# A decoder layer on one core: shorter ways at five places, and the merge's gates loaded ahead

## The chip, the core and the metric

The kernel runs on one core of one Trainium2 chip. A core has five engines, each with its own list of instructions that it takes in order: TensorE (PE, matmuls into the PSUM banks), VectorE (DVE), ScalarE (ACT), GpSimd (POOL, which here works on SBUF only) and SyncE (SP, which here issues most of the transfers). Engines wait for one another by semaphores. The metric is the device time of one execution in microseconds (us).

## The reference

One decoder layer over 1,024 tokens of width 1,024, in float32. Two mixers read the same normalised input: sparse attention over 8 heads (a compressed, a selected and a sliding-window branch) and gated linear attention (GLA) over 4 heads. Their outputs are projected, gated and summed, and a gated channel mixer follows. Cut to what matters here:

```python
h = rmsnorm(x, norm_mix[layer])
proj = h @ w_in[layer]
q_nsa, kv_nsa, g_nsa, q_gla, k_gla, v_gla, lr_gla, r_gla, g_merge = split_in_proj(proj)
k_cmp = compress_blocks(kv[0], ...)          # and v_cmp
o_a = nsa_attention(q_a, k_cmp, v_cmp, kv[2], kv[3], kv[4], kv[5], gates_a)
o_b = gla_chunked(q, k, v, log_a)            # then rmsnorm, times silu(r_gla)
gate_a, gate_b = jnp.split(jax.nn.sigmoid(g_merge), 2, axis=-1)
merged = gate_a * (o_a @ w_up_nsa[layer]) + gate_b * (o_b @ w_up_gla[layer])
x = x + merged @ w_out[layer]
h = rmsnorm(x, norm_ffn[layer])
x = x + (jax.nn.silu(h @ w_ffn_gate[layer]) * (h @ w_ffn_up[layer])) @ w_ffn_down[layer]
return rmsnorm(x, norm_final)
```

## The kernel before

Everything is held transposed: channels on the 128 partitions, tokens along the free dimension, in two halves of 512 tokens (`hf`). Each float32 product of the projections is three matmuls over a high and a low part of each operand (`wh`, `wl`, `hh`, `hl`): high by high, high by low, low by high. A weight tile `wf` is loaded by SP, ACT copies its high part to `wh`, and POOL subtracts to get `wl` (`part` and `half_weights`, L351 to L364); three such tiles are held at a time. `products` (L401) is one such product over the eight or four blocks of 128 channels, and L410 its matmul.

**Order.** PE's list is written by hand, in program order. The lists of the other engines are set at build time by a scheduler, from estimated times; instructions inside `keep_in_program_order` keep their place. A `Fill` is a queue of small items (a product of three matmuls, cost 648 for eight-channel blocks, or a load with cost 0), which the stages take from in between their own work.

**Stages, in order of time.**

1. *Head, to about 173 us.* The input comes in and is split; PE begins with the first columns of queries and keys of GLA. The sum of squares of every token is formed by matmuls with a matrix of ones, and its inverse root `rbc` has one token per column, the same on all partitions (`first_roots`, L571, with `rms_root`). `root_turned` (L579) makes `rtok`, with tokens on the partitions, by eight products of one row by a single one. `rtok` scales the values and the GLA inputs that have tokens on partitions, from about 112 us on. Behind the first projections come the compression jobs: DVE sums a bias `pb` over sixteen blocks of the weights `w1` (L627, L629), and `hidden` multiplies (L638).
2. *GLA, to about 300.* Eight chunks of 128 tokens. For each, `gla_prep` makes decayed copies for seven levels (POOL subtracts, ACT exponentiates, DVE multiplies into `xq`, L828), `gla_diag` the diagonal, `gla_level` a level (PE L859, into one of three banks; DVE copies from it under a mask, L861). `gla_stream` yields a cost after each, and the loop at the end takes fill items for that cost times `ratio`, which spreads the whole fill over the stream.
3. *Sparse attention, 366 to about 777.* 16 units of two groups by eight query blocks, group 0 from the last block down, group 1 upwards. `Plan` writes PE's order by hand from estimated ready times: scores, turns of the weights, value products, with fill in the gaps. All of a unit's value products collect in the one bank `o` (L1165, L1182). `finish` (L1188) copies its upper half to SBUF on ACT (`fo`, L1195), and DVE adds lower half and copy into `oa` (L1197). In `Plan`, `self.o` is when the bank is expected to be free. The fill here is 14 merge-gate projections (stored to `zd`) and five of the eight projections of GLA's output (`UP`, stored to `ud`).
4. *Merge, 783 to about 848.* For eight blocks `m` and two halves: 12 matmuls where `m` is in `UP`, else 24. The evacuation (L1269) loads the two gate halves `za` and `zb`, and `u` where `m` is in `UP`, takes the sigmoid (L1276, L1277), multiplies and adds (L1279 to L1283), and splits the sum into high and low part (`mg`, L1285 and L1286). Then the output projection and the channel mixer follow.
5. *Channel mixer, to the end.* At the end, the last half of the tokens comes in two parts of 320 and 192 columns: `plus` adds the products to the residual (L1588), `square` and `roots` make the last inverse root, and `store` scales (L1602) and stores.

Buffers are rings by tag. `big` has 18 buffers of 4 KB a partition, `prob` 4 of 4 KB, and `mid` 10 of 2 KB.

## Time and profile before

| | us |
|---|---|
| median of three timed runs | 1596.46 |
| the three runs | 1596.6, 1596.46, 1591.89 |
| the profiled execution | 1600.53 |
| its span, first to last instruction | 1598.7 |
| PE busy in the span | 1567.5 (98%) |
| DVE, ACT, POOL busy | 1010.4, 814.4, 678.3 |
| granted clock of PE, mean | 0.998 of full speed |

The profile is of one execution, which took 4.1 us more than the median of the timed runs. A busy PE is one with a matmul under way; what it waits for is found from the semaphores. Times in rows are microseconds from the span's start, unless a column says ns.

### The profile page before, as it was taken

What the parts mean: (1) busy time and instruction counts of PE and PEld (TensorE: products, weight loads), DVE (VectorE), ACT (ScalarE), POOL (GpSimd) and SP (SyncE); (2) the same over time, 40 slices, a digit from 0 to 9 for tenths busy, and PEclk for the clock granted to TensorE, in tenths of its full rate; (3) what the DMA queues carried; (4) which work ended last, traced back from release to release, by engine and by line L of the source; (5) the groups of instructions that cost most, each with busy time, mean ns of one, the idle gap of its engine ahead of it and who ended that gap; (6) DMA issues with size and microseconds to landing.
All of it is one profiled execution on the core that took longest, in us unless ns stands there. A gap on an engine that the chain in (4) does not pass through costs nothing.

```text
span 1598.7 us, 23059 instructions
## 1 busy us (share of the span) xinstructions
PE 1567.5 (98%) x8047; PEld 1311.5 (82%) x8047; DVE 1010.4 (63%) x1653; ACT 814.4 (51%) x1632; POOL 678.3 (42%) x590
## 2 busy tenths in 40 slices
PE   9999999999999999999999999999999999999998
PEld 7888988888888888888877878888888888888887
DVE  7681487586777677677564477744444444499785
ACT  6241555575676676677653344433433444454542
POOL 6110366562212233130144440466666666556570
PEclk9999999999999999999999999999999999999999
DMA  5431112232112122131466532323323323695423
GB/s 182 132 102 61 60 53 68 96 106 83 46 52 65 62 77 65 45 109 60 138 210 206 192 116 73 119 99 106 104 101 105 105 99 99 240 362 162 140 72 125
DMA packets 109590, 179.85 MB, mean 112 GB/s; under 512 B 12689, under 2 KB 29730, under 8 KB 109474
## 3 DMA queue, kind: packets, MB, share of 16 engines
q1 hardware_dynamic: 105442, 171.95, 32.8%
q10 hardware_dynamic: 4032, 6.44, 1.1%
q8 instruction: 63, 1.03, 0.3%
q14 instruction: 53, 0.43, 0.1%
HBM read 128.27 MB, written 45.88 MB: 109 GB/s over the span
## 4 chain that ended last, share of the span: by engine, by line
PE 82%; DVE 6%; DMA 4%; ACT 3%; issue 3%; POOL 2%; SPq 0%; DVEq 0%; POOLq 0%; ACTq 0%
PE m L410 12%; PE d L410 10%; PE m L1397 9%; PE m L1398 9%; PE m L1396 9%; PE m L1759 4%; PE m L1760 4%; PE m L1758 4%; PE o L1182 3%; PE t L1173 3%; PE s L1094 2%; PE s L1095 2%; PE t L725 1%; PE t L726 1%; PE t L727 1%
## 5 line engine op out<-in xcount | busy, mean ns | idle before, releaser
L357 POOL TENSOR_TENSOR wl<-wf,wh 128x512 fp32r<-128x512 f32 x106 | 145.1, 1371 | 323.7 <-ACT wh L356 312.5
L1396 PE MATMUL m<-xt,wh 128*128 128x512 f32 x412 | 160.3, 389 | 0.0
L1397 PE MATMUL m<-xt,wh 128*128 128x512 f32 x412 | 160.3, 389 | 0.0
L1398 PE MATMUL m<-xt,wl 128*128 128x512 f32 x412 | 160.3, 389 | 0.0
L1326 POOL TENSOR_TENSOR wl<-ws,wh 128x512 fp32r<-128x512 f32 x76 | 107.5, 1419 | 73.4 <-ACT wh L1325 73.4
L1151 DVE TENSOR_TENSOR ptl<-t,pth 128x512 fp32r<-128x512 f32 (+1 forms) x168 | 99.4, 596 | 35.5 <-ACT pth L1150 32.5
L1326 POOL TENSOR_TENSOR wl<-wr,wh 128x512 fp32r<-128x512 f32 x69 | 92.2, 1337 | 69.6 <-ACT wh L1325 69.6
L1325 ACT ACTIVATE wh<-ws 128x512 fp32r<-128x512 f32 x76 | 48.0, 632 | 131.4 <-PE m L1397 114.7
L1150 ACT ACTIVATE pth<-t 128x512 fp32r<-128x512 f32 (+1 forms) x168 | 88.0, 525 | 52.8 <-PE t L1173 46.9
L1325 ACT ACTIVATE wh<-wr 128x512 fp32r<-128x512 f32 x87 | 55.0, 632 | 116.9 <-POOL wl L1326 76.4
L1758 PE MATMUL m<-xb,wh 128*128 128x512 f32 x280 | 109.5, 391 | 0.3 <-DVE g L1458 0.3
L1759 PE MATMUL m<-xb,wh 128*128 128x512 f32 x280 | 109.0, 389 | 0.0
L1760 PE MATMUL m<-xb,wl 128*128 128x512 f32 x280 | 108.9, 389 | 0.0
L1326 POOL TENSOR_TENSOR wl<-wd,wh 128x512 fp32r<-128x512 f32 x56 | 82.8, 1482 | 58.3 <-ACT wh L1325 54.7
L410 PE MATMUL m<-hh,wh 128*128 128x512 f32 x240 | 100.4, 419 | 0.0
L1326 DVE TENSOR_TENSOR xb<-ar,xb 128x512 fp32r<-128x512 f32 x73 | 80.3, 1117 | 31.8 <-ACT xb L1325 31.8
L410 PE MATMUL m<-hh,wl 128*128 128x512 f32 x240 | 93.8, 391 | 0.0
L410 PE MATMUL m<-hl,wh 128*128 128x512 f32 x240 | 93.7, 390 | 0.0
L356 ACT ACTIVATE wh<-wf 128x512 fp32r<-128x512 f32 x106 | 65.9, 625 | 53.6 <-PE m L410 25.1
L1396 PEld LDWEIGHTS m<-xt,wh 128*128 128x128 f32 x412 | 77.3, 188 | 16.2
L1398 PEld LDWEIGHTS m<-xt,wl 128*128 128x128 f32 x412 | 77.3, 188 | 16.0
L1397 PEld LDWEIGHTS m<-xt,wh 128*128 128x128 f32 x412 | 77.3, 188 | 16.0
(414 smaller groups left out, 4545.5 us busy)
## 6 DMA issues: line engine op xcount, KB each, us to landing
ar<-actd SPq DMA_DIRECT2D x77, 256.0 KB, 2.8
wf<-in_w_t SPq DMA_DIRECT2D x58, 256.0 KB, 2.9
wr<-in_w_gate SPq DMA_DIRECT2D x44, 256.0 KB, 2.7
wr<-in_w_upf SPq DMA_DIRECT2D x44, 256.0 KB, 2.7
wd<-in_w_down SPq DMA_DIRECT2D x33, 256.0 KB, 5.2
zd<-zt SPq DMA_DIRECT2D x32, 256.0 KB, 2.0
wf<-in_w_out SPq DMA_DIRECT2D x32, 256.0 KB, 3.2
actd<-t SPq DMA_DIRECT2D x30, 256.0 KB, 2.0
```

Source lines behind the costliest of these rows:

```text
L357: (eng or V).tensor_tensor(wl, wf, f(wh), OP.subtract)
L410: PE.matmul(st["p"], w, x, start=k + i == 0, stop=k == n - 1 and i == 2)
L1150: S.activation(th[:, :c], pt[:, :c], AF.Copy)
L1151: V.tensor_tensor(tl[:, :c], pt[:, :c], f(th[:, :c]), OP.subtract)
L1325: S.activation(th, src, AF.Copy)
L1326: eng.tensor_tensor(tl, src, f(th), OP.subtract)
L1396: PE.matmul(ps, wh[:, c], xh, start=first and k == 0, stop=False, skip_group_check=not first)
L1397: PE.matmul(ps, wh[:, c], xl, start=False, stop=False, skip_group_check=not first)
L1398: PE.matmul(ps, wl[:, c], xh, start=False, stop=k == MH - 1, skip_group_check=not first)
L1758: PE.matmul(dst, wh[:, c], xh, start=first and p == 0, stop=False, skip_group_check=not first)
L1759: PE.matmul(dst, wh[:, c], xl, start=False, stop=False, skip_group_check=not first)
L1760: PE.matmul(dst, wl[:, c], xh, start=False, stop=p == NP - 1, skip_group_check=not first)
```

## The change

Six edits. (1) The first roots come behind seven items of the first work list instead of five; three of these items are loads, so four products stand before them instead of two. (2) `root_turned` stores one partition of `rbc` to memory and loads it back with tokens on the partitions; PE and a PSUM bank have no part in it. (3) In GLA 1,200 is added to the cost behind each diagonal, and to the whole by which `ratio` divides. (4) In `finish`, but for the last unit, DVE copies the lower half of the bank to SBUF beside ACT's copy, and POOL adds the two copies; the planner expects the bank back when the later of the two copies is done. For group 0, POOL also makes the high and low parts of `oa`, before the work of ACT and DVE. (5) In the merge, the gate halves of one block and half come as one load into a tile of the ring `big`, three halves ahead, `u` for both halves of a block as one load into the ring `prob`, and one sigmoid covers both gates, in program order. (6) Three of the eight stores of the second to last part are put behind the last additions.

```diff
@@ -101,7 +101,7 @@
 LAT, WAIT, LOADED, COPIED = 155.0, 300.0, 1500.0, 3000.0
 NBIG, NMID, NSMALL = 18, 10, 8
 SCRATCH = 2048
-FINE, NGATE = 3, 2
+FINE, NGATE, AHEAD = 3, 2, 1200
 
 UP = (1, 2, 4, 5, 7)
 
@@ -212,9 +212,7 @@
         later()
         self.t += 218.0 * n if b.br else 436.0
         if last and b.br == 2 and b.j == 1:
-            t = self.on("A", self.t, 478.0)
-            t = self.on("D", t, 670.0)
-            self.o = t + LAT
+            self.o = max(self.on("A", self.t, 478.0), self.on("D", self.t, 550.0)) + LAT
 
     def run(self):
         ops = dict(T=(self.turn_at, self.turn), S=(self.score_at, self.score), P=(self.value_at, self.value))
@@ -576,11 +574,11 @@
         for n in (2, 3, 4, 5, 0, 1):
             scaled(dst[n], acc[n] if n > 1 else dst[n], n % 2, 0.125 if n < 4 else None)
 
+    rtd = dr.tile([1, T], F32, name="rtd")
+
     def root_turned():
-        ps = ps_o()
-        for b in range(NB):
-            PE.matmul(ps[:, b:b + 1], rbc[0:1, bs(b)], ones[0:1, 0:1], start=True, stop=True)
-        V.tensor_copy(rtok, ps[:, :NB])
+        load(rtd, rbc[0:1, :])
+        load(rtok, rtd.rearrange("o (b p) -> p (o b)", p=128))
 
     def proj(evac, bank=ps_m, fine=False):
 
@@ -733,7 +731,7 @@
     j1, h1, t1, s1 = compress_job(1)
     lb, wb = token_weights(a["w_b"], 512, 2)
     work = dense([(a["w_t"][3], proj(lambda p, hf: scaled(kg[hf][:, 1, :], p, hf))), j0, key_job(0), j1, key_job(1)], ready=first)
-    fill.add(work[:5] + [(900.0, first_roots), (0.0, load_consts)] + work[5:20] + [(400.0, root_turned)] + work[20:48] + h0 + work[48:59] + t0
+    fill.add(work[:7] + [(900.0, first_roots), (0.0, load_consts)] + work[7:20] + [(0.0, root_turned)] + work[20:48] + h0 + work[48:59] + t0
              + work[59:63] + s0 + work[63:69] + lb[:1] + work[69:74] + lb[1:2] + work[74:84] + h1 + lb[2:] + work[84:])
     fill.flush()
 
@@ -909,7 +907,7 @@
     def gla_stream():
         for c in range(NB):
             gla_diag(c)
-            yield 860
+            yield 860 + AHEAD
             for i in range(NLV):
                 gla_level(c, i)
                 yield 430
@@ -952,7 +950,7 @@
         return a["w_t"][8 + 2 * g + j], proj(lambda p, hf: scaled(qr[g][hf][:, j, :], p, hf, 0.125))
 
     fill.add(dense([query_job(0, 0), query_job(0, 1)] + [gate_job(j) for j in range(NGATE)]))
-    ratio = fill.cost() / (8 * (860 + 7 * 430 + 3220) + 1500)
+    ratio = fill.cost() / (8 * (860 + AHEAD + 7 * 430 + 3220) + 1500)
     for cost in gla_stream():
         fill.run(cost * ratio)
     fill.flush()
@@ -1191,12 +1189,18 @@
             hf = i // 4
             if oa[g][hf] is None:
                 oa[g][hf] = big("oa", shape=(2, 512))
-            fo = mid("fo")
+            fo, end = mid("fo"), (g, i) == units[-1]
             S.activation(fo[0:64, :], po[64:128, :], AF.Copy)
+            if not end:
+
+                t = mid("fp")
+                tc.keep_in_program_order(V.tensor_copy(t[0:64, :], po[0:64, :]))
+                po = t
             for par in range(2):
-                V.tensor_add(oa[g][hf][64 * par:64 * par + 64, :, bs(i % 4)],
-                             po[0:64, :].rearrange("p (j r q) -> p j r q", j=2, r=2)[:, :, par, :],
-                             fo[0:64, :].rearrange("p (j r q) -> p j r q", j=2, r=2)[:, :, par, :])
+                (V if end else P).tensor_tensor(
+                    oa[g][hf][64 * par:64 * par + 64, :, bs(i % 4)],
+                    po[0:64, :].rearrange("p (j r q) -> p j r q", j=2, r=2)[:, :, par, :],
+                    fo[0:64, :].rearrange("p (j r q) -> p j r q", j=2, r=2)[:, :, par, :], OP.add)
             del UN[g, i]
 
 
@@ -1249,11 +1253,32 @@
         for j in range(2):
             th, tl = big("oah", F32R), big("oal", F32R)
             for hf in range(2):
-                S.activation(th[:, hs(hf)], oa[g][hf][:, j, :], AF.Copy)
-                V.tensor_tensor(tl[:, hs(hf)], oa[g][hf][:, j, :], f(th[:, hs(hf)]), OP.subtract)
+                if g:
+                    S.activation(th[:, hs(hf)], oa[g][hf][:, j, :], AF.Copy)
+                else:
+                    P.tensor_copy(th[:, hs(hf)], oa[g][hf][:, j, :])
+                (V if g else P).tensor_tensor(tl[:, hs(hf)], oa[g][hf][:, j, :], f(th[:, hs(hf)]), OP.subtract)
             oah.append(th)
             oal.append(tl)
+
+
+    fetched, US = {}, {}
+    halves = deque((m, hf) for m in range(NM) for hf in range(2))
+
+    def fetch():
+        if halves:
+            m, hf = halves.popleft()
+            t = big("zz", shape=(2, 512))
+            SP.dma_start(t, zd.rearrange("(a m) p t -> m p a t", a=2)[m][:, :, hs(hf)])
+            if m in UP and hf == 0:
+                US[m] = prob("u")
+                SP.dma_start(US[m], ud[m])
+            fetched[m, hf] = t, US.get(m)
+
+    for _ in range(2):
+        fetch()
     fill.flush()
+    fetch()
 
 
     psum("pp3", m=7, o=1)
@@ -1267,16 +1292,12 @@
                     ps[hf] = p
 
                 def evac(p, hf=hf):
-                    za, zb = mid("za"), mid("zb")
-                    SP.dma_start(za, zd[m, :, hs(hf)])
-                    SP.dma_start(zb, zd[8 + m, :, hs(hf)])
+                    zz, u = fetched.pop((m, hf))
+                    za, zb = zz[:, 0, :], zz[:, 1, :]
+                    fetch()
+                    tc.keep_in_program_order(S.activation(zz, zz, AF.Sigmoid))
                     if m in UP:
-                        u = mid("u")
-                        SP.dma_start(u, ud[m, :, hs(hf)])
-                    S.activation(za, za, AF.Sigmoid)
-                    S.activation(zb, zb, AF.Sigmoid)
-                    if m in UP:
-                        P.tensor_tensor(zb, u, zb, OP.mult)
+                        P.tensor_tensor(zb, u[:, hs(hf)], zb, OP.mult)
                     else:
                         V.tensor_mul(zb, ps[hf], zb)
                     V.tensor_mul(za, za, p)
@@ -1596,10 +1617,12 @@
         else:
             sums[n].append(sq)
 
-    def store(blk, mp, hf, c=slice(0, 512)):
+    def store(blk, mp, hf, c=slice(0, 512), late=False):
         m = mp + (MH if blk[0] == "2" else 0)
         xv, at = x1[blk, mp][:, c], slice(512 * hf + c.start, 512 * hf + c.stop)
-        V.scalar_tensor_tensor(xv, xv, gains[:, 2, m:m + 1], rbc[:, at], op0=OP.mult, op1=OP.mult)
+        ins = V.scalar_tensor_tensor(xv, xv, gains[:, 2, m:m + 1], rbc[:, at], op0=OP.mult, op1=OP.mult)
+        if late:
+            tc.keep_in_program_order(ins)
         (S if c.start and mp % 2 else SP).dma_start(outT[:, m, at], xv)
 
 
@@ -1717,7 +1740,9 @@
         when(i + 2, roots, 0, H[h])
         when(i + 2, sums[0].__delitem__, slice(1, None))
         for k in range(2 * MH):
-            when(i + 5 + k // 2, store, "12"[k // MH] + "1", k % MH, 0, H[h])
+
+            late = h == 0 and k > MH
+            when(i + (NP - ALL + 2 if late else 5 + k // 2), store, "12"[k // MH] + "1", k % MH, 0, H[h], late)
 
     with tc.manual_schedule(engines={mybir.EngineType.SP}):
         for i in range(3):
```

SP's list at the head, behind the input's loads. `wf` are weight tiles, `cst` the constants, `w` and `pe` the compression weights. Before:

```order
L355 DMA wf<-in_w_t 128x512 x3
L497 DMA cst_471<-in_consts 128x768
L497 DMA cst_476<-in_consts 128x448
L610 DMA w_573<-in_cmp_w 128x1024
L610 DMA w_574<-in_cmp_w 128x1024
L497 DMA w_577<-in_cmp_w 128x128
L497 DMA pe<-in_cmp_pe 128x16
L355 DMA wf<-in_w_t 128x512 x2
```

With the change:

```order
L353 DMA wf<-in_w_t 128x512 x4
L495 DMA rtd<-rbc 1x1024
L495 DMA cst_478<-in_consts 128x768
L495 DMA cst_483<-in_consts 128x448
L495 DMA rtok<-rtd 128x8x1
L608 DMA w_566<-in_cmp_w 128x1024
L608 DMA w_567<-in_cmp_w 128x1024
L495 DMA w_570<-in_cmp_w 128x128
L495 DMA pe<-in_cmp_pe 128x16
L353 DMA wf<-in_w_t 128x512
```

One weight load has moved ahead of the constants, and the store and the load of the root stand before and behind them; the compression weights come after both.

SP's list where the attention ends and the merge begins. `zd` and `ud` are the stored gates and projections, `za`, `zb`, `zz` and `u` their tiles. Before:

```order
L355 DMA wf<-in_w_up 128x512
L1215 DMA ud<-zt 128x512
L1271 DMA za<-zd 128x512
L1272 DMA zb<-zd 128x512
L1271 DMA za<-zd 128x512
L1215 DMA ud<-zt 128x512
L1272 DMA zb<-zd 128x512
L1271 DMA za<-zd 128x512
L1272 DMA zb<-zd 128x512
L1275 DMA u<-ud 128x512
L1271 DMA za<-zd 128x512
L1272 DMA zb<-zd 128x512
```

With the change:

```order
L353 DMA wf<-in_w_up 128x512
L1272 DMA zz<-zd 128x2x512
L1219 DMA ud<-zt 128x512
L1272 DMA zz<-zd 128x2x512
L1275 DMA u<-ud 128x1024 x3
L1272 DMA zz<-zd 128x2x512 x4
L1219 DMA ud<-zt 128x512
L353 DMA wf<-in_w_up 128x512
L1219 DMA ud<-zt 128x512
L1275 DMA u<-ud 128x1024
L353 DMA wf<-in_w_up 128x512
```

Six gate loads and three of `u`, of 512 KB each, now stand before the next weight load.

POOL's list in the last units of the attention. `qa`, `qb` and `qs` prepare a unit's queries, `obl` is a low part of GLA's output. Before:

```order
L1236 TENSOR_TENSOR obl<-obf,obh 128x512
L357 TENSOR_TENSOR wl<-wf,wh 128x512
L1035 TENSOR_TENSOR qa<-qa,qb 128x256
L1236 TENSOR_TENSOR obl<-obf,obh 128x512
L357 TENSOR_TENSOR wl<-wf,wh 128x512
L1045 TENSOR_TENSOR qs<-qq,qs 128x2x256
L357 TENSOR_TENSOR wl<-wf,wh 128x512 x5
```

With the change:

```order
L355 TENSOR_TENSOR wl<-wf,wh 128x512
L1200 TENSOR_TENSOR oa<-fp,fo 64x2x128 x2
L1259 CAST oah<-oa 128x512 x2
L1043 TENSOR_TENSOR qs<-qq,qs 128x2x256
L355 TENSOR_TENSOR wl<-wf,wh 128x512
L1260 TENSOR_TENSOR oal<-oa,oah 128x512 x2
L1259 CAST oah<-oa 128x512 x2
L355 TENSOR_TENSOR wl<-wf,wh 128x512
L1200 TENSOR_TENSOR oa<-fp,fo 64x2x128 x2
L1260 TENSOR_TENSOR oal<-oa,oah 128x512 x2
L355 TENSOR_TENSOR wl<-wf,wh 128x512 x5
```

Each pair of additions and the four pairs for `oah` and `oal` stand between weight splits; in the units before, a pair of additions stands in the list likewise, once a unit.

## Rows read from the trace of the kernel before

**Rows 1.** The page, part 1: busy us, share of the span, instructions.
```profile
PE 1567.5 (98%) x8047; PEld 1311.5 (82%) x8047; DVE 1010.4 (63%) x1653; ACT 814.4 (51%) x1632; POOL 678.3 (42%) x590
```
**Rows 2.** Timeline of PE around the first roots: start, us, instruction [idle before].
```profile
40.89 0.49 PE L573 MATMUL o<-ssh,onesr 128*128 128x512 f32 x1 [1.12 <-ACT ssh L568]
41.62 0.50 PE L574 MATMUL o<-ssl,onesr 128*128 128x512 f32 x1 [0.23 <-DVE ssl L569]
...
42.55 0.39 PE L410 MATMUL m<-hh,wh 128*128 128x512 f32 x1
```
**Rows 3.** Timeline of PE at the turned root and the first compression matmuls.
```profile
51.87 0.39 PE L410 MATMUL m<-hh,wl 128*128 128x512 f32 x1
52.19 1.94 PE L582 MATMUL o<-ones,rbc 1*128 1x1 f32 x16
...
71.50 7.22 PE L638 MATMUL m<-w,kst 128*63 128x128 f32 x64 [0.15 <-issue]
```
**Rows 4.** Timeline of SP's queue, 49 to 72 us.
```profile
51.54 2.90 SPq L355 DMA_DIRECT2D wf<-in_w_t  x2
```
**Rows 5.** Transfers of the whole run: count, KB each, median us to landing.
```profile
za<-zd SPq DMA_DIRECT2D x16, 256.0 KB, 3.5
...
w<-in_cmp_w SPq DMA_DIRECT2D x4, 512.0 KB, 6.4
...
ggain<-in_gla_norm SPq DMA_DIRECT2D x1, 0.5 KB, 3.2
```
**Rows 6.** Timeline of DVE, 49 to 72 us.
```profile
49.68 0.68 DVE L438 SCALAR_TENSOR_TENSOR rbc<-nv,nq 128x512 f32<-128x512 f32 x1
...
59.83 1.41 DVE L617 TENSOR_TENSOR kst<-m,rbc 64x512 f32<-64x512 f32 x2 [3.07 <-PE m L410]
...
70.71 0.69 DVE L544 TENSOR_TENSOR krt<-m,rbc 128x512 f32<-128x512 f32 x1 [2.82 <-PE m L410]
```
**Rows 7.** Waits of PE, 173 to 300 us: us, times, longest.
```profile
PE t L859 <- DVE xq L828: 2.3, 4, 0.8
PE t L859 <- DVE at L861: 2.1, 2, 1.6
```
**Rows 8.** Timeline of DVE in one chunk of GLA.
```profile
259.83 2.49 DVE L828 TENSOR_TENSOR xq<-xx,qz 128x256 f32<-128x256 f32 x4
```
**Rows 9.** Waits of PE, 366 to 783 us.
```profile
PE t L1173 <- DVE rr L1105: 1.9, 1, 1.9
PE o L1165 <- DVE oa L1197: 1.7, 2, 1.2
```
**Rows 10.** DVE by line and shape, 366 to 783: busy us, mean ns, idle before.
```profile
L1197 DVE TENSOR_TENSOR oa<-o,fo 64x256 f32<-64x256 f32 x32 | 13.3, 414 | 5.6 <-ACT fo L1195 5.2
```
**Rows 11.** POOL by line and shape, 366 to 783.
```profile
L357 POOL TENSOR_TENSOR wl<-wf,wh 128x512 fp32r<-128x512 f32 x34 | 44.8, 1319 | 134.9 <-ACT wh L356 131.0 <-ACT qs L1044 3.9
...
L1033 POOL TENSOR_TENSOR qa<-qr,rp 128x256 f32<-128x256 f32 x15 | 11.1, 738 | 50.9 <-DMA rp<-in_rope 50.8
```
**Rows 12.** Waits of PE, 783 to 865 us.
```profile
PE m L410 <- POOL wl L357: 2.6, 3, 1.3
PE m L410 <- ACT wh L356: 2.0, 2, 1.4
```
**Rows 13.** Timeline of ACT, 829 to 860 us.
```profile
846.72 0.63 ACT L1277 ACTIVATE zb<-zb 128x512 f32<-128x512 f32 x1 [3.69 <-DMA zb<-zd]
...
847.78 1.13 ACT L356 ACTIVATE wh<-wf 128x512 fp32r<-128x512 f32 x2
```
**Rows 14.** DVE by line and shape, 783 to 865: busy us, mean ns, idle before.
```profile
L1283 DVE TENSOR_TENSOR za<-za,zb 128x512 f32<-128x512 f32 x16 | 15.6, 977 | 0.7
...
L1282 DVE TENSOR_TENSOR za<-za,m 128x512 f32<-128x512 f32 x16 | 10.8, 678 | 0.0
```
**Rows 15.** Timeline of DVE at the end, 1584 to 1596 us.
```profile
1585.15 3.79 DVE L1602 SCALAR_TENSOR_TENSOR x<-x,gains,rbc 128x320 f32<-128x320 f32 x8
1588.85 1.14 DVE L1588 TENSOR_TENSOR x<-x,m 128x192 f32<-128x192 f32 x4
```

## The prediction

> **What bounds the kernel now.** I read the page's busy times first, then what TensorE (PE) waits for, stage by stage. PE is busy 98% of the span [rows 1]: nothing on another engine pays unless it ends a wait of PE. So the change is worth the PE waits that it ends and the PE instructions that it removes, less the waits that it makes. Its places lie in five stages, and each is read from its own stage.
>
> - Head (to 120 us): PE waits 1.12 and 0.23 us for the sum of squares [rows 2], and later spends 1.94 us on sixteen one-element instructions [rows 3].
> - Gated linear attention (GLA, 173 to 300): three kinds of wait, 2.3 and 2.1 us [rows 7] and one of 0.3, 4.7 together.
> - Sparse attention (366 to 783): five kinds of wait, 6.8 us together; the reader sees the longest, and the 1.7 us for the output bank [rows 9].
> - Merge and the start of the output projection (783 to 865): PE waits for split weights, 2.6 and 2.0 us [rows 12], and with two smaller rows for merged halves, 0.9 together, 5.5.
> - Tail: VectorE (DVE) does eight final scalings in 3.79 us before the last additions can begin [rows 15].
>
> **Part 1, first roots two products later.** Six matmuls now precede the roots' four. In this stretch matmuls start 0.227 us apart (from 42.55 to 51.87 there are 41 steps, [rows 2, 3]), so six take 1.36 us. PE idled from about 39.6 to 40.89. It now arrives at 41.0, still waits for the second half of the sum, which came at 41.62, and the roots' group ends at 42.55 as before, with 1.36 us of work done ahead of it. Gain 1.36. The inverse roots come at the same time, so nothing behind them is later.
>
> **Part 2, the turned root through memory.** The sixteen instructions go: 1.94 us [rows 3]. In their place two transfers stand in SP's queue, and they have a price. The store waits for the whole root row, which DVE finished at 50.36 [rows 6], and stands behind one more weight load, which was issued at 51.54 [rows 4]. The constants' loads come behind the store, and the compression weights behind the load of the turned root, which waits for the store. I time it so: store at 50.5, landed 2 us later (an estimate, below the 3.2 us of the smallest load shown, [rows 5]); compression weights issued at 53 to 54, landed 6.4 us later [rows 5]; and 0.6 us for the turned root's 1,024 single elements ahead of them, an estimate whose only row is the 128-element load of 0.5 KB with 3.2 us to landing. DVE's chain of sixteen small steps over these weights then starts near 61, some 6 us later than before. It had 3.07 and 2.82 us of idle time there [rows 6], and the key half that follows it in DVE's order would be evacuated about 0.5 us late, with the compression's matmuls behind. Parts 1 and 2: 1.36 + 1.94 − 0.5 = 2.8. Bounds: 3.3 (all hidden) and −1.0 (the weights land 4 us later than I say, and PE waits for all of it).
>
> **Part 3, GLA.** Two products instead of one stand between a chunk's diagonal and its first level; the fill's total is the same, so they are missing elsewhere. The first level waited for DVE's factors four times, at most 0.8 us [rows 7], and one more product is 0.68. But the second level needs the next factor, and these leave DVE 0.62 us apart (four in 2.49, [rows 8]), faster than a fill product but slower than a level alone; so about 0.4 of each wait comes back there. I take 1.0. Bounds: 4.7 (no wait left) and −2.1 (the wait for the level's bank twice as long, with less fill around it).
>
> **Part 4, the output bank.** ScalarE (ACT) and DVE now copy the two halves of the bank at once, and GpSimd (POOL) adds them later. Before, DVE idled 5.2 us in the stage for ACT's copy and then did two additions of 0.414 us a unit [rows 10], before the bank was free. Both of PE's waits for it, 1.7 us, go. As the planner is told of the earlier release, it lists the attention's work in another order, and the other 5.1 us of waits, where engines run off the plan, are drawn anew. POOL gets 30 additions over half the partitions (nearest row 0.738 us, [rows 11]) and 8 operations of about 1.3, 33 us in 417; its cover is idle time, 134.9 us before weight splits alone [rows 11]. I take +1.5. Bounds: +6.8 (no wait left) and −4.0 (the waits drawn anew nearly twice as long as they were).
>
> **Part 5, the merge's gates.** This is the largest term. Before, each half's loads are issued in its evacuation, and ACT, in order, waits for them: at 846.72 it had waited 3.69 us for one gate half, and the two weight copies at 847.78 stood behind it [rows 13], without which PE could not go on. Now gate pairs lie in large buffers that the attention has left, three halves ahead by the code and up to six by SP's order, and one sigmoid covers both gates. A half takes PE 12 or 24 matmuls, 2.7 or 5.4 us, so three halves are over 8 us, against loads of 3.5 [rows 5]. ACT no longer waits for gates, and the weight copies come when their buffers are free. Of 5.5 us I take 4.6; what may stay is DVE's chain at the last halves, where an addition takes 977 ns in the mean [rows 14]. Bounds 5.5 and 0.5.
>
> **Part 6, late stores.** Three of eight scalings, 3.79/8 = 0.47 us each, move behind the last additions, which started at 1588.85 [rows 15]. PE's last products end near 1589.3 and its sums of four squares stand behind them in any case, so of 1.4 us only about 0.3 reach the end: +0.3.
>
> **Sum.** 2.8 + 1.0 + 1.5 + 4.6 + 0.3 = 10.2 us. The profiled execution took 1600.53 (span 1598.7 and 1.8 around it), which would become 1590.3. It lies 4.1 above the median of the three timed runs, 1596.46; by that median the time is 1586.3, and that is my forecast. The bounds' distances from the terms, added by squares, are 9 us towards slower and 7 towards faster. The three runs differ by 4.7. The range is 1578.5 to 1595.5. About 0.3%, 4.8 us, is what a measurement of this kernel can tell from no change.
>
> **Rivals.**
> *B, the burst of loads.* In SP's new order nine loads of 512 KB stand nearly in a row ahead of the next weight load. Two such loads side by side took 6.4 us to land [rows 5], so nine may take up to 29 (4.5 such pairs), and a weight behind them lands 20 us or more into the merge, when PE is about to ask for it, with its copy and its split of 1.3 to come. For it: the order. Against: in the old order nine loads of 256 KB stand as close, and the merge's first weights are loaded before either burst. It would leave 1.5 of 4.6: gain 7.1, 1589.4.
> *C, the port of DVE and POOL.* The additions moved to POOL slow DVE. In the merge DVE's addition of two SBUF tiles took 977 ns in the mean, its product with one input in a PSUM bank 678 [rows 14], so 0.3 us may be lost where POOL runs beside. If each of 15 units loses one such 0.3 us on a chain that PE waits for, and the waits drawn anew eat what the bank gave, 4.5 + 1.5 go: gain 4.2, 1592.3. For it: POOL's work in this stage grows by a third. Against: DVE's commonest operation there has an input in PSUM.
> The Trainium skill (SBUF — State Buffer, Who interferes with whom) states this rule: a DVE instruction with two SBUF inputs contends with a GpSimd instruction that reads SBUF, and the later one is blocked for the whole of the other. The two means just given agree with it.
> *D, slower: POOL's queue.* POOL takes its list in order, and each pair of additions now stands ahead of weight splits. Where ACT's or DVE's copy is later than planned, POOL stands before the addition, and the split behind it is late. It decides from 10.2/15 = 0.68 us a pair on; at 1.0 each it takes 15, a loss of 4.8: 1601.3. For it: the order. Against: from 366 to 783 PE did not wait for a split once (it is not among the five kinds), since three are held ready, and POOL idled 134.9 us before its splits [rows 11].
> *That the change does not do what it says* would show as gate loads held until their buffers come free; by the order they wait only for the end of the attention, so this is no case of its own but part of B.
>
> **Chances.** Forecast 0.60, B 0.16, C 0.17, D 0.07. Faster by over 0.3%: 0.93 of the forecast, 0.7 of B and a fifth of C, 0.71. Slower by over 0.3%: D, 0.07. Within: 0.22.
>
> **What would show it.** The sixteen one-element instructions and the wait of 1.12 us gone, and the first compression matmul, now at 71.50 [rows 3], near 68.7 (later than 70.5: part 2 cost more than I say). In GLA, waits for DVE's factors at half of 2.3 us. In the sparse attention no wait for the output bank, and splits still not waited for (a row of over 5 us: D). From 783 on no ACT wait for gate loads, and PE's waits at 1 us instead of 5.5 (waits for weights in the first 25 us: B). The forecast is wrong if the merge gives under 2 us, or if PE's waits in the sparse attention grow by more than 4.

## The result, and the profile after

The changed kernel takes 1582.17 us (median of six runs, 1581.46 to 1583.87). Before takes 1596.53 (median of six, 1591.89 to 1600.96). The ratio is 0.9913, 95% interval 0.9896 to 0.9930: 14.4 us by the medians, where 10.2 were forecast. The profiled execution of the changed kernel took 1581.73, near its median; that of before had lain 4.0 above its own. So the spans differ by 19.0 us and not by 14.4.

The page, part 1, of the changed kernel (busy us, share of the span, instructions), beside [rows 1]:

```profile
span 1579.7 us, 23000 instructions
PE 1559.4 (99%) x8031; PEld 1310.5 (83%) x8031; DVE 1009.6 (64%) x1633; ACT 809.6 (51%) x1612; POOL 708.5 (45%) x628
```

PE has 16 instructions fewer, those that turned the root; POOL has 30 us more of work. What PE still waits for in the whole run (us, times, longest), of the changed kernel:

```profile
PE m L636 <- issue: 2.6, 2, 2.1
PE s L1092 <- ACT p L1123: 2.2, 1, 2.2
PE t L857 <- DVE xq L826: 1.6, 2, 0.8
PE t L1171 <- DVE ptl L1149: 1.5, 3, 1.1
PE m L408 <- POOL wl L355: 1.4, 1, 1.4
PE d L486 <- DVE warm L483: 1.3, 1, 1.3
PE t L857 <- DVE vs L748: 0.9, 1, 0.9
PE o L1163 <- DVE fp L1197: 0.3, 1, 0.3
PE d L871 <- DVE at L859: 0.3, 1, 0.3
PE o L572 <- DVE ssl L567: 0.2, 1, 0.2
```

Of the rows of before, the two for the merge's weights [rows 12], the one for `rr` and the one for the output bank [rows 9], and the one for `at` [rows 7] are gone or down to 0.3 (the 1.4 for `wl` lies behind the merge). Most has grown the first row, 2.1 us at the first compression matmul, where before had 0.15 [rows 3]. The wait for `p` went from 1.7 to 2.2 us, and the one for `vs`, 0.9, is new.

The spans split at PE instructions that both kernels have (starts read from the timelines of PE; each stretch ends where the next begins):

| stretch of PE | before | changed | gain | forecast |
|---|---|---|---|---|
| start to the first root's matmul | 40.9 | 40.4 | 0.5 | 0 |
| to the first compression matmul | 30.6 | 29.0 | 1.6 | 2.8 |
| to the first mean after GLA | 237.1 | 233.9 | 3.2 | 1.0 |
| to the first attention score | 60.1 | 60.1 | 0 | 0 |
| attention, to the first product with `oah` | 419.8 | 416.4 | 3.4 | 1.5 |
| merge, to the sum of squares behind it | 112.8 | 104.7 | 8.1 | 4.6 |
| to the feed-forward's first matmul | 43.1 | 42.0 | 1.1 | 0 |
| to the last sum of squares | 613.9 | 613.2 | 0.7 | 0 |
| to the end | 40.5 | 40.0 | 0.5 | 0.3 |

The 0.5 at the start and the 1.1 and 0.7 near the end are not the change's: in the twelve kernels below these stretches scatter by as much (the first from 40.5 to 41.5, the seventh from 41.2 to 44.1, the eighth from 613.3 to 614.1), whatever is changed in them. The merge's stretch comes out alike to 0.02 us in all kernels with fetched gates.

**The head.** SP's queue of the changed kernel, from 35 us (start, us, instruction):

```profile
35.07 15.03 SPq L353 DMA_DIRECT2D wf<-in_w_t  x4
50.33 0.24 SPq L495 DMA_DIRECT2D rtd<-rbc  x1
50.62 1.49 SPq L495 DMA_DIRECT2D cst<-in_consts  x2
52.38 0.38 SPq L495 DMA_DIRECT2D rtok<-rtd  x1
52.80 1.44 SPq L608 DMA_DIRECT2D w<-in_cmp_w  x2
...
54.76 0.43 SPq L495 DMA_DIRECT2D pe<-in_cmp_pe  x1
```

The fourth weight load waits for its buffer to 49.8, and the rest stands behind it. Before, that load waited too, to 51.54 [rows 4], but the compression weights had gone ahead of it, in SP's queue of the kernel before:

```profile
40.49 0.86 SPq L610 DMA_DIRECT2D w<-in_cmp_w  x2
...
41.87 0.44 SPq L497 DMA_DIRECT2D pe<-in_cmp_pe  x1
```

VectorE's timeline of the changed kernel shows what follows:

```profile
55.81 1.41 DVE L615 TENSOR_TENSOR kst<-m,rbc 64x512 f32<-64x512 f32 x2 [0.19 <-PE m L408]
60.04 0.40 DVE L625 TENSOR_SCALAR pb<-w,pe 128x128 f32<-128x128 f32 x1 [2.82 <-DMA pe<-in_cmp_pe]
...
65.91 2.68 DVE L627 SCALAR_TENSOR_TENSOR pb<-w,pe,pb 128x128 f32<-128x128 f32 x7
68.62 0.69 DVE L542 TENSOR_TENSOR krt<-m,rbc 128x512 f32<-128x512 f32 x1
```

The chain `pb` starts at 60.04, and the evacuation of the key half, `krt`, stands behind its last seven steps. It ends at 69.31; PE, whose next work needs that bank, goes on at 69.41. In all fourteen profiles PE begins this work 0.10 us behind the end of `krt`:

```profile
69.41 0.78 PE L636 MATMUL m<-w,kst 128*63 128x128 f32 x5 [2.08 <-issue]
```

**The merge.** ACT's waits from 779 to 847 us in the changed kernel, where 846.72 and its like stood before [rows 13]:

```profile
ACT mg L1306 <- DVE zz L1304: 28.4, 16, 3.7
ACT wh L354 <- POOL zz L1300: 1.4, 1, 1.4
ACT wh L354 <- POOL wl L355: 1.1, 1, 1.1
...
```

No gate load is among them, nor in the smaller rows left out. ACT's waits from 783 to 848 us before:

```profile
ACT za L1276 <- DMA za<-zd: 15.4, 12, 3.5
ACT zb L1277 <- DMA zb<-zd: 8.3, 7, 3.7
...
```

PE waits for nothing at all from 779.7 to 884.5.

### The profile page after: what moved, and what is told of

It is laid out like the page before. It is cut to its first block, busy times and chain, and to the rows that moved or that the text cites. A ratio compares the mean times of both kernels' runs of the same rounds, so it can differ in the third digit from the quotient of the medians.

```text
span 1579.7 us, 23000 instructions
## 1 busy us (share of the span) xinstructions
PE 1559.4 (99%) x8031; PEld 1310.5 (83%) x8031; DVE 1009.6 (64%) x1633; ACT 809.6 (51%) x1612; POOL 708.5 (45%) x628
## 4 chain that ended last, share of the span: by engine, by line
PE 90%; DVE 4%; DMA 2%; ACT 2%; issue 1%; POOL 1%; SPq 0%; DVEq 0%; ACTq 0%; POOLq 0%
PE m L408 17%; PE d L408 10%; PE m L1419 9%; PE m L1418 9%; PE m L1417 9%; PE m L1784 4%; PE m L1783 4%; PE m L1785 4%; PE o L1180 3%; PE t L1171 3%; PE s L1092 2%; PE s L1093 2%; PE t L723 1%; PE t L724 1%; PE t L725 1%
```

## Experiments

Each is the changed kernel, or before, with the edit shown. Ratios are to runs of before on the same chip, with their 95% intervals. By those the twelve kernels can be told from before but hardly from each other, since 0.0015 either way is 2.4 us; so the stretches above decide, read from one profile of each.

One thing moves these stretches whatever is edited: the clock that PE is granted. In seven of the fourteen profiles it falls from 2.4 to 1.2 GHz for 3.4 us in the attention, just behind PE's wait for `p` at 575 to 581 us. A stretch of 3 us behind that wait in the changed kernel (stretch, us, busy us of PE, PEld, DVE, ACT and POOL, granted clock as a share of 2.4 GHz, share and GB/s of the DMA engines):

```profile
577.50:580.50 3.00, 3.00 (x9) 2.32 (x8) 2.79 (x9) 2.19 (x9) 2.01 (x4) 0.50 0.16 41
```

and the like in the kernel without GLA's extra fill:

```profile
581.20:584.20 3.00, 3.00 (x18) 2.50 (x17) 2.86 (x10) 2.96 (x11) 2.02 (x4) 1.00 0.14 37
```

From the end of that wait to the matmul 25 places on, PE takes 5.88 to 5.90 us in the five profiles with the change's order of PE, the wait and the fall, and 4.30 to 4.32 in the five without the fall: it costs 1.6 us there. It is in the profiles of before, the changed kernel, the merge alone, the kernel without part 5, the turned root on PE, the compression weights written ahead and the last kernel. The others have the wait too (but for the additions on VectorE) and no fall; what decides it is open.

Ahead of GLA it fell in three profiles: behind a wait of 3.0 us, told below; with the splits on VectorE at 71 us; and in the merge alone right behind the sixteen one-element instructions. That kernel's head is the one of before, and from the roots to the compression it took 32.2 us instead of 30.6. So the head's gain of 1.6 rests on two single profiles.

**The merge by itself, and the change without it.** First: before with the gates fetched as in the diff and nothing else.

```diff
-                    za, zb = mid("za"), mid("zb")
-                    SP.dma_start(za, zd[m, :, hs(hf)])
...
+                    zz, u = fetched.pop((m, hf))
+                    za, zb = zz[:, 0, :], zz[:, 1, :]
+                    fetch()
...
```

> Before with part 5 alone (gate pairs in large tiles, three halves ahead, one sigmoid). Measure: PE's stretch from the first product of the merge's own rows (obh, oah at 788.45 before) to the sum of squares (901.26): 112.8 us before, 104.7 with the whole change. Theory M, the gain is the merge's own, since gate loads no longer stand ahead of weight copies in ACT's order: 104.5 to 106, PE waits in it under 0.5 us, and the time 7 to 8 us below before (ratio 0.995 to 0.9955). Rival N, part of it comes from the other parts (GpSimd preparing the first group's operand, an earlier end of the attention): 107 to 110, ratio 0.9965 to 0.998.

Second: the changed kernel with the gates loaded in each half's evacuation again.

```diff
-                    zz, u = fetched.pop((m, hf))
-                    za, zb = zz[:, 0, :], zz[:, 1, :]
-                    fetch()
-                    tc.keep_in_program_order(S.activation(zz, zz, AF.Sigmoid))
+                    za, zb = mid("za"), mid("zb")
+                    SP.dma_start(za, zd[m, :, hs(hf)])
+                    SP.dma_start(zb, zd[8 + m, :, hs(hf)])
...
```

> The changed kernel without part 5 (gates loaded in each half's evacuation, as before); all other parts stay. Theory M: the merge's stretch is back at 111 to 114 us, ACT waits for gate loads again, and the rest keeps its gain: 7 us below before, ratio 0.995 to 0.9965. Rival N: the stretch stays at 107 to 110 us, ratio 0.9925 to 0.994.

The merge alone: stretch 104.73 us, as with the whole change; attention 419.8, as before; 1591.42 against 1597.98, ratio 0.9957 (0.9943 to 0.9970). Theory M holds on that side: 6.6 us, a little under its 7 to 8, and the gain needs no other part. Without it: stretch 109.69, ratio 0.9944 (0.9931 to 0.9957). ACT waits for gate loads again as M says, 14.8 us for `za` and 8.4 for `zb`, but the stretch lies in N's range and the ratio between N's and M's. PE's waits are of the same kinds as before, but smaller, so the loss may simply vary from run to run. PE's waits in that stretch of the kernel without part 5, beside [rows 12]:

```profile
PE m L408 <- POOL wl L355: 1.3, 2, 0.6
PE m L408 <- ACT wh L354: 1.1, 2, 0.6
PE m L408 <- ACT mg L1294: 0.4, 1, 0.4
PE m L408 <- DVE mg L1295: 0.2, 1, 0.2
```

With one profile of each it is not excluded that the other parts shorten the stretch by 3 us where the gates are not fetched (N). Where they are, the other parts add nothing, since the merge alone reaches 104.73.

**Buffers or place in the program.** The changed kernel with the gates fetched at the same places, in the small buffers of before:

```diff
-            t = big("zz", shape=(2, 512))
-            SP.dma_start(t, zd.rearrange("(a m) p t -> m p a t", a=2)[m][:, :, hs(hf)])
+            za, zb, u = mid("za"), mid("zb"), None
+            SP.dma_start(za, zd[m, :, hs(hf)])
+            SP.dma_start(zb, zd[8 + m, :, hs(hf)])
...
```

> The changed kernel with the gates still fetched three halves ahead in the program, but into the ten half-size buffers that before used, in separate loads of 256 KB and two sigmoids. Theory B1, the buffers decide: a load still waits for a half's tiles to come free, so ACT waits for gate loads again and the merge's stretch takes 108 to 112 us. Rival B2, the place in the program decides: under 106, as with the change (104.7).

The stretch took 104.73 us, and PE waited for nothing in it: B2. ACT's waits from 779 to 847 us in this kernel, where no load stands either:

```profile
ACT mg L1307 <- DVE za L1305: 26.9, 15, 3.5
...
```

Neither the large tiles nor the joint sigmoid is worth anything measurable (ratio 0.9917, 0.9900 to 0.9934). What counts is that the loads are written ahead, or that the sigmoids keep their place in ACT's order, which this kernel has from the change as well: no run tells these two apart.

**GLA's extra fill: 0 and 2400 for 1200.**

```diff
-FINE, NGATE, AHEAD = 3, 2, 1200
+FINE, NGATE, AHEAD = 3, 2, 0
```

> The changed kernel with the extra fill after each diagonal set to 0, as before. Measure: PE's stretch from the first q by x transposition product of the linear attention to the first mean (190.68 to 308.63 before: 117.95 us; 113.99 with the change). Theory F, the one extra product does it: 117 to 118 us, waits of 4 to 5 us, time 3 to 4 us above the changed kernel. Rival G, the waits fell by chance (other phase of loads and of the other engines after the head): 114 to 116 us.

> The changed kernel with 2400 in place of 1200 as the extra fill after each diagonal. The linear attention took 117.9 us at 0 and 114.0 at 1200. Theory F, each step of a product ends waits where PE has too little to do after the diagonal: the four waits left (2.5 to 2.8 us) fall to under 1, 112 to 113 us. Rival K, what is taken elsewhere comes back as waits at the levels: 114 to 116 us.

At 0 the stretch from GLA's first transposition to the first mean is 117.92 us, as before (117.95), at 1200 it is 113.99, at 2400 112.15. Ahead of it 0.7 us come back at each step, so the net gains are 3.2 and 1.2 more. F's stretches hold both times; its time at 0, 3 to 4 us above the changed kernel, came out 2.4 above, and its waits at 2400, under 1 us, at 1.1. PE's waits from 173 to 310 us, first at 0:

```profile
PE t L857 <- DVE xq L826: 2.3, 4, 0.8
PE t L857 <- DVE at L859: 2.1, 2, 1.6
PE t L857 <- POOL xx L830: 0.3, 1, 0.3
```

These are the rows of before to the tenth [rows 7], though the head is another: the waits are set by the order and not by chance. And at 2400:

```profile
PE t L857 <- DVE xq L826: 0.5, 2, 0.3
PE d L871 <- DVE at L859: 0.4, 1, 0.4
PE t L857 <- DVE vs L748: 0.2, 1, 0.2
```

The times follow: 1584.56 at 0 (ratio 0.9920, 0.9906 to 0.9934) and 1579.79 at 2400 (0.9881, 0.9865 to 0.9896), with the last kernel below the fastest, and 2.4 us below the change, whose interval its own just touches.

**The attention.** Three edits of the changed kernel. The planner told the old release of the output bank:

```diff
-            self.o = max(self.on("A", self.t, 478.0), self.on("D", self.t, 550.0)) + LAT
+            t = self.on("A", self.t, 478.0)
+            t = self.on("D", t, 670.0)
+            self.o = t + LAT
```

> The changed kernel, but the planner is told the old, later release of the output bank; the copies and GpSimd's additions stay. It tells the two halves of part 4 apart in the attention (368.7 to 788.45 before: 419.75 us; 416.4 with the change). Theory O, the faster release itself is worth the 1.7 us of waits for the bank and the planner's new order the rest: 418 us, no wait for the output bank. Rival Q, the gain is nearly all the new order's, waits drawn anew: 419.5 us or more, and other waits than the bank's. Rival R, all is the release's: 416.5.

The additions on VectorE:

```diff
-                (V if end else P).tensor_tensor(
+                V.tensor_tensor(
```

> The changed kernel with the two additions per unit on VectorE and not on GpSimd; the bank is still freed by two copies side by side. Theory O, the early release and the first group's splits on GpSimd are what the attention gained from, and the additions' engine is nearly free: the attention takes 415 to 417.5 us (414.8 to 416.8 in the runs of the change's finish), no wait for the output bank over 0.4. Rival C, GpSimd's additions slow VectorE by the shared port: 413 to 414.5. Rival V, VectorE's relief by 0.8 us a unit is the gain: 418 to 420, as before (419.75).

The first head group's operand split by ACT and VectorE, as before:

```diff
-                if g:
-                    S.activation(th[:, hs(hf)], oa[g][hf][:, j, :], AF.Copy)
-                else:
-                    P.tensor_copy(th[:, hs(hf)], oa[g][hf][:, j, :])
-                (V if g else P).tensor_tensor(tl[:, hs(hf)], ...
+                S.activation(th[:, hs(hf)], oa[g][hf][:, j, :], AF.Copy)
+                V.tensor_tensor(tl[:, hs(hf)], ...
```

> The changed kernel with the first head group's output operand split by ScalarE and VectorE again, as before, not by GpSimd; the bank's copies and additions stay as changed. Before, PE waited 1.88 us at 734.46 for a reciprocal rr, and VectorE had two splits of oal (1.46 and 0.68 us) just ahead of it. Theory S, these splits in VectorE's order are that wait: it comes back near the same place (1.5 to 2.5 us), the attention takes 417.5 to 418.5 us (416.4, 416.0 and 415.1 in runs of the change's finish, 419.75 before). Rival T, the wait went since the release of the bank drew the order anew: no wait for rr, 415 to 416.5.

The two kernels with the old finish (before and the merge alone) took 419.8 us in the attention, both with the fall of the clock. The twelve in which two copies free the bank, the changed kernel and eleven edits, took 414.8 to 417.0. The five of them with the fall took 416.4 in the mean, which is a gain of 3.4; the seven without it took 414.8 to 416.7.

With the old plan it was 414.83, without a fall (ratio 0.9901, 0.9887 to 0.9915), and PE's order in the attention is that of before, instruction by instruction. So the planner's number is worth nothing that can be seen, and the faster release works without a new order: R.

With the additions on VectorE it was 416.74, without a fall (ratio 0.9906, 0.9888 to 0.9924). That lies in O's range and above C's. But the other kernels without a fall whose splits are on POOL took 414.8 to 416.2, in the mean 415.3, and V's 418 to 420 was taken from a profile with one. So VectorE's relief may be worth up to some 1.5 us; the time does not show it, and O is not settled against V.

With the splits back on VectorE the wait for `rr` came back, 1.9 us as before. VectorE's timeline of that kernel shows the cause:

```profile
727.16 1.46 DVE L1257 TENSOR_TENSOR oal<-oa,oah 128x512 fp32r<-128x512 f32 x1
...
729.27 0.68 DVE L1257 TENSOR_TENSOR oal<-oa,oah 128x512 fp32r<-128x512 f32 x1
...
730.21 0.15 DVE L1103 RECIPROCAL rr<-z 128x1 f32<-128x1 f32 x1
```

The two splits take 2.1 us in the order ahead of the reciprocal that PE stands for. This is S for the wait's cause. The stretch was 416.35 and not 417.5 to 418.5 (ratio 0.9922, 0.9904 to 0.9941), since this profile lacks the fall of the clock that the changed kernel's has. Its price shows step by step: from six matmuls ahead of that wait to six behind it PE takes 3.43 us here, and 1.37 in all ten other kernels with the same order of PE. So the wait's cause is shown, and it costs 2.1 us.

**The head.** What makes the compression weights late? First the constants moved ahead of the two added products; then the turned root on PE again.

```diff
-    fill.add(work[:7] + [(900.0, first_roots), (0.0, load_consts)] + work[7:20] + ...
+    fill.add(work[:5] + [(0.0, load_consts)] + work[5:7] + [(900.0, first_roots)] + work[7:20] + ...
```

> The changed kernel with the constants' loads written ahead of the two products that part 1 puts before the first roots, so that SP issues them before the fourth weight load, near 39 us and not 50.6. PE's wait of 2.08 us before the first compression matmul is in question. Theory H, volume behind the weight load: 0.6 MB of constants and 1.1 MB of compression weights leave the queue in one go after 49.8 us, and with the constants gone the weights land near 57 and not 60: wait under 0.5, the stretch from the first root's matmul to the compression 27.1 to 27.6 us (29.0 with the change), time 1.5 to 2 us below the changed kernel. Rival E, the 1,024 single elements of the turned root hold the queue: they stay, so the wait stays above 1.5.

```diff
-        load(rtd, rbc[0:1, :])
-        load(rtok, rtd.rearrange("o (b p) -> p (o b)", p=128))
+        ps = ps_o()
+        for b in range(NB):
+            PE.matmul(ps[:, b:b + 1], rbc[0:1, bs(b)], ones[0:1, 0:1], start=True, stop=True)
+        V.tensor_copy(rtok, ps[:, :NB])
```

> The changed kernel with the root turned by the sixteen one-element matmuls again (part 2 undone, part 1 kept). Theory H: the loads still stand behind the fourth weight load, so most of the wait before the compression stays beside the 1.94 us of the matmuls (they only push it later): roots to compression 29.0 to 30 us, the sum no better than with the change. Rival E: without the element load the compression weights land 2 us earlier, and the stretch is 29.0 (1.94 more work and no wait), equal to the change: then the wait itself is under 0.3.

Both fall short. In the eight kernels with the change's head the chain began between 59.58 and 60.92, the stretch took 28.3 to 29.1 us, and the wait was 2.08 or 2.09 us in seven and 2.43 in one. With the constants gone at 39.3 us the chain still began at 58.75, and PE waited 1.7, and 0.4 for `kg` besides (stretch 29.13, ratio 0.9915, 0.9894 to 0.9936): the volume is not it, H fails, while E's "above 1.5" came true. With the turned root on PE the chain began at 59.38, and PE waited 0.9 beside its 1.94 of matmuls (stretch 29.98, in H's range; ratio 0.9922, 0.9905 to 0.9939): the element load is not it, E fails. In both the compression weights still stood behind the fourth weight load. So they were written ahead of it themselves:

```diff
+    loads = []
...
+    fill.add(work[:5] + [(0.0, load_consts), (0.0, loads[0])] + work[5:7] + [(900.0, first_roots)] + ...
```

(`loads[0]` issues the four loads that the evacuation issued.)

> The changed kernel with the constants' loads and the first compression's weight loads both written ahead of the two added products, so that SP issues them before the fourth weight load and before the store of the root row (both of which wait until about 50 us). Moving the constants alone left a wait of 1.7 us, taking out the turned root alone one of 0.9. Theory W, the compression weights are late because they stand behind an SP row that waits to 50 us, whichever it is: now they land before 50 us, VectorE's chain over them starts by 56, PE's wait before the compression is under 0.5 us, roots to compression 27.0 to 27.6 us (29.0 with the change), time 1.5 to 2 us below the changed kernel. Rival X, VectorE is simply full there, or the key half's bank is late for another cause: the wait stays above 1.2.

The weights were issued at 40 to 42 us, and the wait before the compression fell to 0.15: W is right about it. But the stretch got longer, 33.11 us from the roots to the compression, and the time, ratio 0.9917 (0.9903 to 0.9931), is no better than the change's. PE's waits from 40 to 80 us:

```profile
PE m L408 <- DVE kg L542: 3.0, 1, 3.0
...
PE m L643 <- issue: 0.2, 1, 0.2
```

and VectorE's timeline of this kernel:

```profile
42.82 0.23 DVE L341 CAST mdb<-cst 128x128 bf16<-128x128 f32 x1 [1.18 <-DMA cst<-in_consts]
...
43.74 0.68 DVE L432 TENSOR_SCALAR nv<-o 128x512 f32<-128x512 f32 x1
...
47.14 0.28 DVE L632 TENSOR_SCALAR pb<-w,pe 128x128 f32<-128x128 f32 x1 [0.72 <-DMA pe<-in_cmp_pe]
...
48.26 1.82 DVE L436 SCALAR_TENSOR_TENSOR rbc<-nv,nq 128x512 f32<-128x512 f32 x1
...
52.70 0.68 DVE L542 TENSOR_TENSOR kg<-m,rbc 128x512 f32<-128x512 f32 x1
```

k's bank came free at 53.4, where PE had asked for it at 50.4. This `kg` ended 4.2 us later than in the changed kernel (49.20). The chain was now free to go early, and two of its steps, with the wait for `pe`, stand among the root's and k's: some 1.5 us. The casts of the constants, early as well, put the root's first step to 43.74, where the changed kernel has it at 42.31: 1.4. And one half of the root took 1.82 us instead of 0.68, beside a weight split of POOL: 1.1.

The wait of 3.0 explains only part of the longer stretch. Behind it the granted clock is 0.50 from 53 to 59 us, and PE's matmuls start 0.43 us apart instead of 0.227: 2.9 us more. So 29.0 less 1.9, with 3.0 and 2.9 added, makes 33.0 of the 33.1.

**Both repairs.** The last kernel holds the chain behind the first roots in the program, and takes 2400 for GLA:

```diff
+    fill.add(work[:5] + [(0.0, load_consts), (0.0, loads[0])] + work[5:7] + [(900.0, first_roots), (0.0, loads[1])] + ...
```

(`loads[1]` is the chain, its first step kept in program order.)

> The changed kernel with 2400 as the extra fill after each diagonal, and with the head mended: the constants and the first compression's weights are loaded ahead of the fourth weight load, and VectorE's chain over them is held in the program behind the first roots, so that it stands behind the evacuations of k and not between them (that had made PE wait 3.0 us for kg). Theory W: no wait for kg, the wait before the compression under 0.5 us, roots to compression 27.0 to 27.8 us (29.0 with the change), the linear attention 112.2 with 77.1 ahead of it as with 2400 alone, and 1.5 to 2 us below the run with 2400 alone (ratio 0.9881 to before), so 0.9865 to 0.9875. Rival X, the chain finds no place on VectorE there that PE does not wait for: head at 28.5 us or more, ratio 0.988 or above.

From the roots to the compression it takes 27.60 us: the head's 1.4 us are won. PE's waits from 40 to 104 us:

```profile
PE m L646 <- issue: 1.3, 2, 1.1
PE m L408 <- DVE kg L542: 0.4, 1, 0.4
```

W's "no wait for `kg`" is missed by the 0.4, which the kernel with the constants alone moved has too. The second group of compression matmuls now waits 1.1 us where it had waited 0.6, and the attention took 417.0 us in that profile, with a fall of the clock (1.6 us) that the profile of 2400 alone has not. The time is 1579.88, ratio 0.9885 (0.9868 to 0.9901), the same as with 2400 alone. W holds in its stretch, and its time does not show.

## Why the prediction was right, and where its terms were off

The direction and the range held, and the largest term was the largest; but parts 1 and 2, second in the forecast, came out fourth. The sum of 10.2 was low against 14.4, from three terms that were too small and one that was too large, whose surplus hid some of the others' lack, which is luck. Between the two profiles the terms add to 16.6; with part 5 at the 6.6 of its timed runs, to 15.1.

- **Part 5, 4.6 forecast.** The mechanism was as said: no wait of ACT for gate loads, and the weight copies on time. The size was 6.6 us in the timed runs of that part alone and 8.1 between the two profiles. I had taken the sum of the listed waits, 5.5, as the upper bound and held 0.9 of it back for DVE's chain. Nothing was left over. And a listed wait is less than what it costs. A matmul lasts 0.39 us and the next one starts after 0.227 [rows 2]; the wait is counted from the end of the first, so 0.16 us of the standstill are not in it. In the profile of before the merge's seven waits sum to 5.4 us, while the starts around them lie 6.7 further apart than steps of 0.227. Behind each wait the next step was 0.11 longer, which no row lists.
- The Trainium skill (TensorE: Matmul & The Clock Gate, Step-by-step: what each phase is for) says that in a stream one matmul's drain overlaps the next one's fill, and an isolated one pays for it. This case's trace agrees: 0.16 to 0.28 us beyond each listed wait in the merge.
- **Part 3, 1.0 forecast.** 3.2. The step that failed: only the waits for DVE's factors were priced, and the 2.1 us for the level's bank stood there as a risk alone. They went (1.6 of them a single wait, at 247.82 before), and 0.3 is left at another place. Of the 2.3 for the factors just 0.7 went, by none of the reasoning: two of the four waits ended whole, and the other two did not shrink (0.82 and 0.63 before, 0.85 and 0.79 after). "About 0.4 of each wait comes back" is so wrong in kind; nor does 1.0 follow from it, since 2.3 less four times 0.4 is 0.7. A wait for POOL (0.3) ended too, and one for `vs` (0.9) is new. The listed waits fell by 1.9; the other 1.3 of the stretch is in no listed wait.
- **Part 4, 1.5 forecast.** The bank's two waits went, as said. What I counted as drawn anew and worth nothing contained a wait with a cause in the diff: `rr`, behind two splits on VectorE that part 4 gives to POOL. I had priced these eight operations on POOL's side only. 3.4 between the two profiles, and in the mean of those with a fall of the clock. The order that the planner draws anew was worth nothing, as forecast.
- **Parts 1 and 2, 2.8 forecast.** 1.6. The chain's start was right (near 61; it was 60.04), and so was the way by which it costs, a key half evacuated late. Its price of 0.5 was 1.93 (2.08 against 0.15): the seven steps of 0.38 us that now stand ahead of that evacuation are 2.7 us, where before had one, and I had asked for the lag of the chain's start, not for what of the chain stands between the second `kst` and `krt`. Nor had I counted that parts 1 and 2 bring PE itself to this half earlier: the matmul that `krt` waits for began at 70.28 before and at 66.27 after, so the idle 2.82 us that were to hide the lag were gone. No run shows the 0.6 us put down for the 1,024 single elements by themselves; without them, and with PE later by its 1.94, the wait was 0.9. The first compression matmul came at 69.41, between the 68.7 forecast and the 70.5 that I had named as too late.
- **Part 6, 0.3 forecast.** From the last sum of squares to PE's last instruction 32.95 us before and in the merge alone, 32.61 to 32.66 in all others: 0.3.
- **Rivals.** B: nine loads stood in a row, and no weight was waited for in the merge. C: VectorE was slowed by POOL in the merge (below), and PE never stood for it; in the attention the additions on VectorE gained nothing. D: PE waited for no split in the attention.

Open: how much of the 112.8 us of the merge in the one profile of before was its own bad luck. That execution took 4.0 us more than the median, and the kernel without part 5 lost only 5.0 and not 8.1.

## What to carry to other kernels

Price a wait at the distance of the starts around it, not at the listed idle time, and ask what stands in the waiting engine's order directly ahead of the releaser: it is often another part of the same change that moves it. When a load is moved, look for the row ahead of it in its queue that waits for a buffer; and when it comes early, look at where its consumer is then put. Where an engine waits in order for transfers, writing them a few steps ahead can be the whole gain (here together with a fixed place for what uses them); larger buffers and joint operations added nothing here. Before two profiles are compared, look at the granted clock in both: here one fall was worth 1.6 us, as much as parts 1 and 2 gained together.

## What the runs showed of the hardware

VectorE's additions of two tiles in SBUF were slowed wherever they began while POOL was at work: eight of the sixteen in the changed kernel's merge, with 1.09 to 1.78 us, where the other eight took 0.68 or 0.69. VectorE by line, 779 to 885 us, changed kernel (count, busy us, mean ns), beside [rows 14]:

```profile
L1304 DVE TENSOR_TENSOR zz<-zz 128x512 f32<-128x512 f32 x16 | 18.2, 1138 | 3.9 <-POOL zz L1300 3.6
...
L1303 DVE TENSOR_TENSOR zz<-zz,m 128x512 f32<-128x512 f32 x16 | 10.9, 679 | 3.0 <-PE m L408 2.5 <-ACT zz L1298 0.5
```

The mean rose from 977 to 1138 ns, while products with an input in a PSUM bank stayed at 679. One of them in VectorE's timeline:

```profile
818.43 1.76 DVE L1304 TENSOR_TENSOR zz<-zz 128x512 f32<-128x512 f32 x1 [0.69 <-POOL zz L1300]
```

and POOL's timeline at the same place:

```profile
818.36 1.28 POOL L355 TENSOR_TENSOR wl<-wf,wh 128x512 fp32r<-128x512 f32 x1
819.61 1.75 POOL L1300 TENSOR_TENSOR zz<-u,zz 128x512 f32<-128x512 f32 x1
```

The addition came 0.07 us behind POOL's split and took 1.08 us more than the shortest of its kind here (0.68); POOL's next operation began beside it and took 0.45 more than the 1.30 of others. The Trainium skill (SBUF — State Buffer, Who interferes with whom) lets the later of two such instructions wait for the whole of the other; the trace agrees, since each of the eight ended 0.55 us after the POOL operation that it met, less than its own 0.68. Both sides lose, and PE, which waited for nothing in this stage, did not show it.
